# Modulation with the weights as stationary float32 blocks and two moving columns

## The chip, the core and the metric

The kernel runs on one core of a Trainium2 chip. A core has TensorE (matrix products, "PE" in the profile; its weight loads are listed apart as "PEld"), VectorE ("DVE"), ScalarE ("ACT"), GpSimd ("POOL") and SyncE ("SP"), which here only issues DMAs. The metric is the device time of one execution in microseconds (us), as a median of several runs.

## The reference, cut to what matters

One layer of a diffusion trunk is applied to 128 context tokens and 2048 grid tokens with the same weights. Each of the two token groups has its own condition vector of 1024 values. The part that the change touches is the modulation: `silu(cond) @ w_ada + b_ada`, with `w_ada` of 1024 x 6144, which gives six vectors of 1024 values for each group.

```python
mod = (jax.nn.silu(cond) @ w_ada + b_ada)[..., None, :]
shift1, scale1, gate1, shift2, scale2, gate2 = jnp.split(mod, 6, axis=-1)
h = rmsnorm(x, g_mix) * (1 + scale1) + shift1
p = h @ w_in
...                     # convolution, gated DeltaNet in two directions, Fourier mix
x = x + gate1 * (mix @ w_out)
h2 = rmsnorm(x, g_ffn) * (1 + scale2) + shift2
gt, up = jnp.split(h2 @ w_gu, 2, axis=-1)
x = x + gate2 * ((jax.nn.silu(gt) * up) @ w_down)
```

So shift1 and scale1 are needed before the first token can be normalised, and the other four only later: shift2, scale2 and gate1 at the end of the mixer, gate2 at the end of the SwiGLU part.

## The kernel before

All products are made to float32 accuracy. The large ones split each operand into a rounded part ("hi", float32r) and the rest ("lo"), and add three float32r products. The splitting is done by `split` (line 145): ScalarE rounds (line 150), and VectorE or, where the caller says so, GpSimd subtracts (line 151, through `tt`, line 130). A helper records each operation, so that nearly all matmuls have line 124, all transposes line 127, all ScalarE operations line 140.

The stages follow each other as functions:

- `setup` (line 188) loads constants and computes `silu(cond)`; it splits the two condition columns into four columns `cs4` (hi and lo of each) and two columns `cs2` padded to four.
- `phase_a` (line 353) is the pass over the tokens. It first runs `mod_columns(0, ...)` (line 367), which calls `mod_part` for shift1 and scale1. Between its steps it calls `load_halves` (line 343), which loads the key half of the input weights, and splits them. Then the 17 blocks of 128 tokens are normalised, transposed (`xn`), modulated to `h`, split to `hi` and `lo`, stored to HBM as `hT` and multiplied with the Fourier and gate columns of the input weights (`wfh`, `wfl`). From the fifth block on the loads and splits go on, one step a block.
- `gates` (line 406) computes the decay gates from all tokens with a few float32 products (`const_gates`).
- `qk_pass` (line 548) goes over 8 blocks of 256 tokens. For each it reloads `hT` (tiles `hb`) and makes 8 projections of 24 matmuls each, then a convolution (ScalarE makes `y` and `conv_in`, VectorE the two taps in `y`, line 137, ScalarE the silu to `kq`), and the products of keys and queries (`pair_products`, line 618, tiles `kq`, `sq`). Behind three of each four projections stands `next(self.mod, None)` (line 577): one step of the later modulation. `self.fill` (line 98) adds steps of the triangular inversion (tiles `inv_a`, `inv_b`, `inv_m`), which VectorE does alone.
- `v_pass` (line 767) does the same for the values and for `z`; there the modulation steps stand at line 782.
- `scan1` and `scan2` walk over the chunks of 64 tokens, and the Fourier part and the output product run beside them.
- `phase_d` (line 1303) is the SwiGLU part in three blocks of up to 768 tokens.

`mod_part` (line 231) handles one of the six vectors. It goes over two halves of 512 columns and, in each, over 8 blocks of 128 rows; one such block of 128 x 512 weights is called a step here, so a vector has 16 steps. A step loads the weights (one DMA for one or two steps, line 243), splits them (line 244), and makes two matmuls in which the condition columns are stationary (128 x 4) and the weights move (512 columns), lines 245 and 246. After 8 steps ScalarE copies the 4 x 512 result to `row`, four small transposes turn it to columns, and ScalarE copies them to `v` (lines 248 to 253). In the head the split weights lie in the tiles of the query half of the input weights (line 363), which is why that half is loaded only afterwards; later they have two tiles of their own, tagged `ada` (line 263), and GpSimd subtracts (line 375).

The order of the instructions on each engine is set by a scheduler that works from the program's order and from a timing model of its own (`schedule_with_timeline_sim=True`, line 1462). Each engine then runs its queue in that order, and a tile that is not free yet holds up the instruction that writes it. The pool `stage` (line 322) has 3 buffers of 4 KB a partition under the tag `st`, which all staged weight loads and `row` share. PSUM has three banks tagged `m` in these phases (line 313).

## Time and profile before

| | us |
|---|---|
| median of 3 runs | 2767.01 (2766.07 to 2773.3) |
| the profiled execution | 2767.64 |
| its span in the profile | 2765.8 |

The rows that the prediction uses stand in the section before it. In the windows, each engine has its busy time and, in brackets, the number of its instructions; PEclk is the granted clock of TensorE as a share of 2.4 GHz, so 0.50 is 1.2 GHz. A matmul is pipelined, so the duration of a single record is longer than its distance to the next, and the busy times of groups overlap. In a group of instructions the last columns are the busy time, the mean duration of one in ns, and the idle time of the engine ahead of them, with what ended it. Names like `acc<-hb,w_in` say what is written and what is read; `m<-w_ada,cs` are the later modulation's matmuls, `m<-w_in,cs` those of the head, whose split weights lie in tiles of `w_in`. A plain float32 matmul is listed as two records.

### The profile page before, as it was taken

Reading aid. Unit: us, or ns where it says so; the run is one execution under the profiler, and the core shown is the slowest. Engines: PE = TensorE matmul, PEld = TensorE weight load, DVE = VectorE, ACT = ScalarE, POOL = GpSimd, SP = SyncE. Lnnn points to the kernel's source line nnn. Section 1 sums busy time; section 2 is a strip of 40 time slices with the busy share of each in tenths; the row PEclk is TensorE's granted clock in tenths of the full one; section 3 lists DMA queues with packets and bytes.
Section 4 is the critical chain, followed back from the end, with each engine's and each line's share of the span. In section 5 each row is a group of like instructions: output and inputs, shape, how many; then the busy total and the mean of one; then the engine's idle time right before and its main releaser. Section 6 shows DMA issues by size and latency. Waiting matters only on the chain.

```text
span 2765.8 us, 44580 instructions
## 1 busy us (share of the span) xinstructions
PE 2610.3 (94%) x15769; PEld 2366.6 (86%) x15769; DVE 1971.7 (71%) x3860; ACT 1395.2 (50%) x3090; POOL 354.4 (13%) x486
## 2 busy tenths in 40 slices
PE   6999798899999899997999999999999999999998
PEld 3898687788888778876999998789999888999987
DVE  6335598998999677755877766577777556888744
ACT  7756454432277877765433344433434444444442
POOL 1214333431200012220000000020000002000001
PEclk8999898899999999998999999999999999999999
DMA  9946685555365666644322223532222253332342
GB/s 311 307 139 204 177 256 162 157 164 180 109 193 194 195 176 195 200 152 151 90 73 73 73 71 94 179 122 77 73 69 70 89 158 120 105 88 82 95 137 93
DMA packets 412283, 390.83 MB, mean 141 GB/s; under 512 B 99948, under 2 KB 335900, under 8 KB 411164
## 3 DMA queue, kind: packets, MB, share of 16 engines
q1 hardware_dynamic: 323996, 300.92, 36.1%
q10 hardware_dynamic: 74128, 40.13, 5.0%
q0 software_dynamic: 13936, 46.93, 4.9%
q8 instruction: 125, 2.05, 0.3%
q14 instruction: 98, 0.80, 0.1%
HBM read 293.55 MB, written 94.33 MB: 140 GB/s over the span
## 4 chain that ended last, share of the span: by engine, by line
issue 31%; PE 27%; DMA 2%; DVE 1%; ACT 1%; POOL 1%; ACTq 0%; POOLq 0%; SPq 0%; DVEq 0%
PE acc L124 9%; PE m L124 8%; PE acc L1273 5%; PE m L1273 5%; PE tr L127 1%; POOL rstd L130 1%; DMA z_s<-z_d 0%; DMA y_f<-half_d 0%; DMA half_d<-gy 0%; DVE x_f L137 0%; ACT h L140 0%; DVE x_f L130 0%; DMA bd1a<-a_d 0%; POOL y L1401 0%; DMA g<-gate_d 0%
## 5 line engine op out<-in xcount | busy, mean ns | idle before, releaser
L1273 PE MATMUL m<-h,wh 128*128 128x384 f32 (+1 forms) x1848 | 456.1, 329 | 14.5 <-ACT h L140 7.2
L1273 PE MATMUL acc<-h,wh 128*128 128x384 f32 (+1 forms) x1848 | 449.8, 327 | 0.0
L140 ACT ACTIVATE wh<-S 128x512 fp32r<-128x512 f32 x264 | 163.8, 630 | 376.5 <-DVE S L130 161.5
L124 PE MATMUL acc<-hb,w_in 128*128 128x258 f32 (+1 forms) x2304 | 333.6, 302 | 15.7 <-DMA hb<-hT 10.9
L1273 PEld LDWEIGHTS m<-h,wh 128*128 128x128 f32 x1848 | 328.4, 189 | 19.6 <-ACT h L140 8.9
L124 PEld LDWEIGHTS acc<-hb,w_in 128*128 128x128 f32 x2304 | 318.3, 199 | 26.8 <-issue 12.2
L1273 PEld LDWEIGHTS acc<-h,wh 128*128 128x128 f32 x1848 | 327.2, 189 | 1.0 <-ACT wh L140 0.4
L1273 PE MATMUL acc<-h,wl 128*128 128x384 f32 (+1 forms) x924 | 300.6, 327 | 6.0 <-DVE wl L130 6.0
L1273 PE MATMUL m<-h,wl 128*128 128x384 f32 (+1 forms) x924 | 302.3, 328 | 0.0
L140 ACT ACTIVATE wh<-w_gu 128x512 fp32r<-128x512 f32 x198 | 124.4, 630 | 118.8 <-issue 51.6
L130 DVE TENSOR_TENSOR wl<-S,wh 128x512 fp32r<-128x512 f32 x264 | 179.0, 686 | 5.3 <-ACT wh L140 3.1
L1273 PEld LDWEIGHTS acc<-h,wl 128*128 128x128 f32 x924 | 174.0, 189 | 6.9 <-DVE wl L130 6.9
L1273 PEld LDWEIGHTS m<-h,wl 128*128 128x128 f32 x924 | 174.9, 189 | 0.0
L140 ACT ACTIVATE awh<-a 128x384 fp32r<-128x384 f32 x176 | 90.7, 520 | 136.0 <-PE m L124 88.1
L130 DVE TENSOR_TENSOR awl<-a,awh 128x384 fp32r<-128x384 f32 x176 | 96.6, 555 | 87.1 <-ACT awh L140 87.0
L1387 POOL DMA_DIRECT2D half_d<-gy x17 | 9.3, 546 | 1160.9 <-DVE gy L130 1160.3
L130 DVE TENSOR_TENSOR wl<-w_gu,wh 128x512 fp32r<-128x512 f32 x198 | 135.4, 685 | 27.2 <-ACT wh L140 27.0
L130 DVE TENSOR_TENSOR S<-w_gu 128x512 f32<-128x512 f32 x132 | 91.1, 691 | 88.4 <-DMA w_gu<-w_gu 87.9
L137 DVE SCALAR_TENSOR_TENSOR y<-conv_in,wconv,y 128x256 f32<-128x256 f32 (+1 forms) x216 | 123.2, 584 | 39.7 <-ACT conv_in L140 39.1
L130 POOL TENSOR_TENSOR w_ada<-w_raw,w_ada 128x512 fp32r<-128x512 f32 x64 | 99.2, 1566 | 136.9 <-ACT w_ada L140 136.7
L124 PE MATMUL acc<-woh,mh 128*128 128x512 f32 x272 | 113.2, 419 | 3.0 <-DVE gx L130 2.9
L130 DVE TENSOR_TENSOR inv_b<-inv_b,inv_m 128x62 f32<-128x62 f32 (+30 forms) x124 | 114.1, 920 | 2.3
(281 smaller groups left out, 5927.9 us busy)
## 6 DMA issues: line engine op xcount, KB each, us to landing
w_gu<-w_gu SPq DMA_DIRECT2D x264, 256.0 KB
pk<-pk_d SPq DMA_DIRECT2D x68, 512.0 KB
w_dn<-w_down SPq DMA_DIRECT2D x132, 256.0 KB
hb<-hT SPq DMA_DIRECT2D x104, 258.0 KB
w_raw<-w_ada SPq DMA_DIRECT2D x32, 512.0 KB
x<-x SPq DMA_DIRECT2D x17, 512.0 KB
hT<-hi ACTq DMA_DIRECT2D x17, 512.0 KB
hT<-lo POOLq DMA_DIRECT2D x17, 512.0 KB, 6.1
```

The source lines that it names most:

```text
L124: self.nc.tensor.matmul(out, lhsT=lhsT, rhs=rhs, start=start, stop=stop)
L127: self.nc.tensor.transpose(out=out, in_=in_, identity=self.c("ident")[:in_.shape[0], :in_.shape[0]])
L130: (eng or self.nc.vector).tensor_tensor(out=out, in0=a, in1=b, op=op)
L137: self.nc.vector.scalar_tensor_tensor(out=out, in0=a, scalar=s, in1=b, op0=op0, op1=op1)
L140: self.nc.scalar.activation(out=out, in_=in_, func=f, **kw)
L1273: nc.tensor.matmul(o, lhsT=w_[:, ws], rhs=h_[:, k, :sub], start=start and k == i == 0, stop=k == 3 and i == 2, skip_group_check=not start)
L1387: nc.gpsimd.dma_start(self.half_d[n], tmp)
```

## The change

The weights are no longer split. Each 128 x 128 block of a step is loaded as it came, as float32, as the stationary operand, and the two condition columns move through it, so a step has four matmuls with two moving columns. The results are columns already: they add up in one PSUM bank for all 16 steps of a vector, which a product with a tile of zeros clears first (a step's matmuls only add). The copies to `row`, the small transposes and `v` fall away, and the columns are read from PSUM. The `ada` tiles are gone, and `stage` has 5 buffers in place of 3. In the head, the weights no longer use the tiles of the input weights, so the loads of both halves no longer stand between the steps or behind them: they are left to the token pass in the program.

```diff
--- before.py
+++ after.py
@@ -190,13 +190,10 @@
         self.cst = {}
         cond = const.tile([P, KT, 2], F32, name="cond")
         nc.sync.dma_start(cond, A["condT"])
-        cs = const.tile([P, KT, 2], F32, name="cs")
-        self.act(cs, cond, AF.Silu)
-        self.cs4 = const.tile([P, KT, 4], F32R, name="cs4")
-        self.cs2 = const.tile([P, KT, 4], F32R, name="cs2")
-        nc.vector.memset(self.cs2.bitcast(F32), 0.0)
-        self.split(self.cs4[:, :, 0:2], self.cs4[:, :, 2:4], cs)
-        nc.vector.tensor_copy(self.cs2[:, :, 0:2], cs)
+        self.cs = const.tile([P, KT, 2], F32, name="cs")
+        self.act(self.cs, cond, AF.Silu)
+        self.none = const.tile([P, 2 * KT], F32, name="none")
+        nc.vector.memset(self.none, 0.0)
         self.load_consts(const, "all")
         self.neg_half = self.small.tile([P, 1], F32, name="neg_half", bufs=1)
         nc.gpsimd.memset(self.neg_half, -0.5)
@@ -228,40 +225,33 @@
         self.h2_d = [d([P, KT, len(b) * P], F32, name=f"h2_d{i}") for i, b in enumerate(BLOCKS)]
         self.gate_d = d([2, 2, D], F32, name="gate_d")
 
-    def mod_part(self, part, tiles, bank, *engs):
+    def mod_part(self, part, raws, bank):
 
         nc, A = self.nc, self.A
-        v = self.small.tile([P, KT, 4], F32, tag="modv", name="modv", bufs=1)
+        ps = self.bank(bank)
+        self.mm(ps[:, :2 * KT], self.c("ident"), self.none)
         for a in range(0, D, 512):
-            ps = self.bank(bank)
             col = part * D + a
             for k in range(KT):
-                hi, lo, raw = next(tiles)
+                raw = next(raws)
                 w = raw.shape[1]
                 if k % w == 0:
                     src = A["w_ada"][k * P:(k + w) * P, col:col + 512]
                     nc.sync.dma_start(raw, src.rearrange("(k p) c -> p k c", p=P))
-                self.split(hi, lo, raw[:, k % w], *engs)
-                self.mm(ps[:4], self.cs4[:, k], hi, start=(k == 0), stop=False)
-                self.mm(ps[:4], self.cs2[:, k], lo, start=False, stop=(k == KT - 1))
+                for n in range(4):
+                    at = 2 * (a // P + n)
+                    nc.tensor.matmul(ps[:, at:at + 2], lhsT=raw[:, k % w, n * P:(n + 1) * P], rhs=self.cs[:, k],
+                                     start=False, stop=True, skip_group_check=True)
                 yield
-            row = self.stage.tile([4, 512], F32, tag="st", name="row")
-            self.act(row, ps[:4])
-            pt = self.bank("tr")
-            for n in range(4):
-                self.tr(pt[:, n * 4:n * 4 + 4], row[:, n * P:(n + 1) * P])
-            self.act(v[:, a // P:a // P + 4].rearrange("p k r -> p (k r)"), pt[:, :16])
         bias = self.b_ada[:, part * KT:(part + 1) * KT].unsqueeze(2).to_broadcast([P, KT, 2])
-        self.tt(v[:, :, 0:2], v[:, :, 0:2], v[:, :, 2:4], ALU.add)
-        return v[:, :, 0:2], bias
+        return ps[:, :2 * KT].rearrange("p (k r) -> p k r", r=2), bias
 
     def ada_tiles(self):
 
         while True:
             raw = self.stage.tile([P, 2, 512], F32, tag="st", name="w_raw")
             for _ in range(2):
-                w = self.stage.tile([P, 2, 512], F32R, tag="ada", name="w_ada", bufs=2)
-                yield w[:, 0], w[:, 1], raw
+                yield raw
 
     def mod_columns(self, which, *source):
 
@@ -319,7 +309,7 @@
     def phase_ab(self):
         nc, A = self.nc, self.A
         with ExitStack() as left:
-            self.stage = self.pool(left, "stage", 3, side="left")
+            self.stage = self.pool(left, "stage", 5, side="left")
             self.wp = self.pool(left, "w_in", side="left")
             wk = self.w_half(1)
             self.hb = self.pool(left, "hb", 16, side="left")
@@ -360,21 +350,17 @@
 
             def tiles():
                 while True:
-                    for hi, lo in zip(*self.w_half(0)):
-                        yield hi, lo, self.hb.tile([P, 1, 512], F32, tag="hb", name="w_raw")
-
-            qk = self.load_halves(wk, 512)
-            for i, _ in enumerate(self.mod_columns(0, tiles(), "m")):
-                if i % 8 == 4:
-                    next(qk)
+                    yield self.hb.tile([P, 1, 512], F32, tag="hb", name="w_raw")
+
+            self.run(self.mod_columns(0, tiles(), "m"))
             wq = self.w_half(0)
             wh = [wp.tile([P, FW], F32R, name=f"wfh{k}") for k in range(KT)]
             wl = [wp.tile([P, FW], F32R, name=f"wfl{k}") for k in range(KT)]
             for k in range(KT):
                 self.load_split(wh[k], wl[k], A["w_in"][k * P:(k + 1) * P, 2048:2048 + FW], FW, self.stage, "st")
-            rest = self.ada_tiles(), "m", nc.gpsimd
+            rest = self.ada_tiles(), "m"
             self.mod = chain(self.mod_columns(1, *rest), self.mod_gate(0, *rest), self.mod_gate(1, *rest))
-            qk = chain(qk, self.load_halves(wq, 0))
+            qk = chain(self.load_halves(wk, 512), self.load_halves(wq, 0))
             for n, t in enumerate([16] + list(range(16))):
                 rows = slice(t * P, (t + 1) * P)
                 x = work.tile([P, D], F32, tag="x", name="x")
```

The order on TensorE at the start. Before (`cs_67` is `cs4` and `cs_68` is `cs2`; the rows are those around the end of the first eight steps):

```order
L124 MATMUL m<-w_in,cs_67 4x512 x2
L124 MATMUL m<-w_in,cs_68 4x512 x2
L124 MATMUL m<-w_in,cs_67 4x512
L127 MATMUL tr<-const_all,row 128x4 x4
L124 MATMUL m<-w_in,cs_68 4x512
```

After, from the first matmul on:

```order
L124 MATMUL m<-none,const_all 128x16 x2
L243 MATMUL m<-cs,w_raw 128x2 x128
L127 MATMUL tr<-const_all,xn 128x128 x12
L124 MATMUL acc<-wfh_352,hi 128x264
L124 MATMUL acc<-wfl_360,hi 128x264
```

All 128 small matmuls of the 32 steps stand in one run ahead of the token pass's transposes.

The order of DMAs on SP in the head, from the first modulation weights on. Before (line 243 modulation weights, 348 halves of the input weights, 278 their Fourier and gate columns, 381 tokens):

```order
L243 DMA w_raw<-w_ada 128x512 x5
L348 DMA w_raw<-w_in 128x2x512
L243 DMA w_raw<-w_ada 128x512 x17
L348 DMA w_raw<-w_in 128x2x512
L243 DMA w_raw<-w_ada 128x512 x9
L381 DMA x<-x 128x1024
L243 DMA w_raw<-w_ada 128x512
L348 DMA w_raw<-w_in 128x2x512
```

After (240 modulation weights, 338 halves, 268 Fourier and gate columns, 367 tokens):

```order
L240 DMA w_raw<-w_ada 128x512 x20
L268 DMA w_raw<-w_in 128x528 x3
L240 DMA w_raw<-w_ada 128x512
L268 DMA w_raw<-w_in 128x528 x2
L240 DMA w_raw<-w_ada 128x512
L367 DMA x<-x 128x1024 x2
...
L338 DMA w_raw<-w_in 128x2x512
L240 DMA w_raw<-w_ada 128x512
L338 DMA w_raw<-w_in 128x2x512 x5
L240 DMA w_raw<-w_ada 128x2x512 x5
```

Twenty modulation loads stand in a row now; the Fourier and gate columns, four token blocks and all eight loads of the halves are mixed with the last twelve or follow them at once, ahead of the first `hT` reloads. On ScalarE and VectorE the 16 splits of the halves now stand ahead of the first modulated token block.

The order on TensorE in the middle of the query and key pass. Before:

```order
L124 MATMUL acc<-hb,w_in 128x258 x14
L124 MATMUL m<-w_ada,cs_67 4x512
L124 MATMUL m<-w_ada,cs_68 4x512
L124 MATMUL acc<-hb,w_in 128x258 x48
L124 MATMUL m<-w_ada,cs_67 4x512
L124 MATMUL m<-w_ada,cs_68 4x512
L124 MATMUL acc<-hb,w_in 128x258 x24
```

After:

```order
L124 MATMUL acc<-hb,w_in 128x258 x23
L243 MATMUL m<-cs,w_raw 128x2 x4
L124 MATMUL acc<-hb,w_in 128x258 x48
L243 MATMUL m<-cs,w_raw 128x2 x4
L124 MATMUL acc<-hb,w_in 128x258 x24
L243 MATMUL m<-cs,w_raw 128x2 x4
```

A step keeps its place behind three of four projections; its two matmuls become four, and they wait for the load alone.

## Rows read from the trace of the kernel before

**Rows 1.** The page's first part: busy time, share of the span, instructions.
```profile
PE 2610.3 (94%) x15769; PEld 2366.6 (86%) x15769; DVE 1971.7 (71%) x3860; ACT 1395.2 (50%) x3090; POOL 354.4 (13%) x486
```

**Rows 2.** Windows: stretch, its length, busy us per engine, PEclk, DMA share, GB/s.
```profile
0.00:46.00 46.00, 27.38 (x93) 8.08 (x94) 29.75 (x57) 34.24 (x67) 1.77 (x9) 0.85 0.87 304
46.00:180.00 134.00, 122.52 (x939) 118.55 (x940) 54.51 (x128) 96.09 (x207) 38.14 (x65) 0.95 0.89 279
180.00:300.00 120.00, 111.99 (x944) 101.75 (x942) 58.16 (x161) 68.39 (x145) 34.65 (x32) 0.99 0.51 152
300.00:880.00 580.00, 519.87 (x3794) 462.62 (x3795) 532.91 (x927) 273.58 (x644) 157.37 (x155) 0.94 0.60 177
1303.00:2750.00 1447.00, 1428.79 (x7763) 1334.21 (x7764) 1002.19 (x1729) 608.49 (x1136) 48.43 (x80) 0.99 0.32 97
```

**Rows 3.** Groups by line, operation and shape: count, busy us, mean ns, idle before.
```profile
L140 ACT ACTIVATE w_ada<-w_raw 128x512 fp32r<-128x512 f32 x64 | 39.0, 630 | 38.3 <-DMA w_raw<-w_ada 27.4 <-PE m L124 8.6 <-DVE r L662 2.0
L130 POOL TENSOR_TENSOR w_ada<-w_raw,w_ada 128x512 fp32r<-128x512 f32 x64 | 99.2, 1566 | 136.9 <-ACT w_ada L140 136.7
L124 PE MATMUL m<-w_ada,cs 128*4 128x512 f32 x128 | 45.5, 418 | 14.4 <-ACT w_ada L140 9.7 <-POOL w_ada L130 4.6
L124 PE MATMUL m<-const_all,sq 128*64 128x1 f32 x544 | 23.1, 206 | 3.0 <-DVE rows L676 2.1 <-ACT sq L140 0.9
L124 PE MATMUL m<-la,const_gates 128*128 128x68 f32 x8 | 1.1, 282 | 1.8 <-DVE la L130 1.8
```

**Rows 4.** The chain that ended last: start us, us, six 512-column matmuls.
```profile
1742.73 1.38 PE acc L124 x6
```

**Rows 5.** Timeline of TensorE: start us, us, operation, stationary rows x columns, moving.
```profile
23.35 0.41 PE L127 MATMUL tr<-const_all,row 4*128 4x4 f32 x4
...
38.03 0.59 PE L127 MATMUL tr<-const_all,row 4*128 4x4 f32 x4 [2.04 <-ACT row L140]
...
208.24 0.83 PE L124 MATMUL m<-la,const_gates 128*128 128x68 f32 x6
```

**Rows 6.** Timeline of three engines in the head.
```profile
6.68 0.63 ACT L140 ACTIVATE w_in<-w_raw 128x512 fp32r<-128x512 f32 x1 [3.75 <-DMA w_raw<-w_ada]
...
41.40 0.17 DVE L130 TENSOR_TENSOR mod_cols<-mod_cols,gains 128x16 f32<-128x16 f32 x1
...
45.74 0.59 PE L124 MATMUL acc<-wfh,hi 128*128 128x264 f32 x1 [0.59 <-ACT hi L140]
```

**Rows 7.** Windows around changes of the granted clock.
```profile
18.55:35.62 17.07, 13.97 (x54) 3.17 (x53) 14.83 (x26) 14.96 (x31) 0.74 (x2) 1.00 1.04 390
35.62:49.27 13.65, 7.76 (x33) 6.17 (x33) 9.88 (x23) 11.92 (x25) 1.77 (x3) 0.50 0.70 219
25.38:28.79 3.41, 2.28 (x8) 0.43 (x7) 3.41 (x7) 3.41 (x8) 0.00 (x0) 1.00 1.05 395
489.58:493.00 3.42, 2.52 (x55) 2.36 (x56) 3.35 (x9) 3.35 (x9) 1.52 (x2) 1.00 0.89 281
493.00:496.41 3.41, 3.41 (x18) 3.41 (x17) 3.41 (x5) 1.45 (x3) 2.92 (x2) 0.50 0.36 109
```

**Rows 8.** Groups by line: 209 to 640, 680 to 755, and 300 to 640 us.
```profile
L137 DVE SCALAR_TENSOR_TENSOR y<-conv_in,wconv,y 128x256 f32<-128x256 f32 x128 | 81.1, 637 | 31.3 <-ACT conv_in L140 31.0
...
L137 DVE SCALAR_TENSOR_TENSOR y<-conv_in,wconv,y 128x256 f32<-128x256 f32 x24 | 11.4, 478 | 0.0
...
L130 POOL TENSOR_TENSOR w_ada<-w_raw,w_ada 128x512 fp32r<-128x512 f32 x48 | 77.3, 1627 | 117.9 <-ACT w_ada L140 117.7
```

**Rows 9.** Timeline of GpSimd and VectorE around 588 us.
```profile
586.99 3.47 POOL L130 TENSOR_TENSOR w_ada<-w_raw,w_ada 128x512 fp32r<-128x512 f32 x2 [17.48 <-ACT w_ada L140]
587.92 2.82 DVE L137 SCALAR_TENSOR_TENSOR y<-conv_in,wconv,y 128x127 f32<-128x127 f32 x2
```

**Rows 10.** Waits, 209 to 680 us: us in total, times, longest.
```profile
ACT kq L140 <- DVE y L137: 58.1, 31, 6.9
...
ACT w_ada L140 <- DMA w_raw<-w_ada: 27.4, 3, 19.9
```

## The prediction

> **What bounds the kernel now.** I read the page's shares first: TensorE is busy 94% of the span [rows 1]. Such a share is a mean over stages, so the second view is the busy time by stretches [rows 2], in which the reader should compare TensorE with VectorE. In 1303 to 2750 us (the SwiGLU part) TensorE is busy 1428.79 of 1447 us and nothing of the change lies there. In 300 to 880 us, VectorE is busy 532.91 of 580 us and TensorE 519.87: two engines share that stretch, and it is where most of the modulation's second share runs. In 0 to 46 us neither is full (27.38 and 29.75 us): that is the head, which waits for the first 32 steps of the modulation. So there are three places to price: the head, the token pass behind it (46 to 180 us), and 180 to 880 us.
>
> **The change part by part.** A step is one 128x512 block of the modulation weights; there are 96, of which 32 in the head and 64 later. *Removed* for each step: one ScalarE rounding copy (0.63 us), one subtraction (VectorE in the head, GpSimd later, 1.57 us there) and two matmuls with 512 moving columns [rows 3]. Such matmuls follow each other every 0.23 us at the full clock (1.38 us for six, [rows 4]), so two cost 0.46 us. Per 8 steps a row copy, four small transposes (0.41 us, [rows 5]) and a copy back go too, and in their place stands one matmul that clears the bank per 16 steps. *Added* for each step: four float32 matmuls with a 128x128 stationary block and 2 moving columns.
>
> No row shows that form. What a float32 matmul is in the trace: line 650 issues 34 x 2 x 4 = 272 of them and the trace has 544 records [rows 3], so each is two load-and-multiply pairs. The nearest row with a full float32 stationary block and few columns is the gates' sums with 68 columns: six records take 0.83 us, the last of them its own 0.28 us, so one starts every 0.11 us [rows 3, 5]. From below: the 64-column blocks with one column take 23.1 us for 544 records, 0.04 us each [rows 3], but they fill half of the array's columns. From above: 0.83/6 = 0.14 us. I take 0.11 us, since that row has the same stationary block and a block with 2 columns must still be loaded. A step then costs 4 x 2 x 0.11 = 0.90 us of TensorE at the full clock against 0.46 us before: +0.44 us (bounds -0.1 and +0.66).
>
> *Head.* The first weights have landed at 6.68 us, when ScalarE begins to split them; the modulation columns are ready at 41.57 us and the first matmul of the token pass starts at 45.74 us [rows 6]. Afterwards the order puts all 128 blocks in one run on TensorE, ahead of everything else. What counts is the clock. Two short stretches of equal length tell: from 25.38 us TensorE was busy 2.28 us with 512-column matmuls and the clock stayed at 2.4 GHz (1.00) until 35.62 us; from 489.58 us it was busy 2.52 us, mostly with kq and sq products of one to 128 columns on half-width blocks, and from 493.00 us it was granted 0.50, which is 1.2 GHz [rows 7]. Being busy with loads did not hold the clock there. A run of 2-column blocks that begins from an idle engine therefore, I take it, stays at the lower level. The four small transposes, nearly all weight load, took 0.59 us at 38.03 us, at that level, and 0.41 us at 23.35 us, at the higher [rows 5, 7], so the load slows with the clock, and I double 0.11 to 0.215 us: 256 records x 0.215 = 55 us, from 6.7 to about 62 us. Transposes, h and its split then take about 3 us (4.2 us before, [rows 6]): the first matmul of the pass at about 65 us, **+19 us**. At the full clock the run would be 28 us and end at 35 us; then the DMAs set the end. What the SP order puts ahead of the pass, about 17 MB (8.4 modulation weights, 2.2 and 4.2 input weights, 2.1 tokens), takes 43 us at the 395 GB/s of a full stretch [rows 7]; with the 6.68 us in which the first of it came, the first matmul would stand at about 50 us: +4 us.
>
> The Trainium skill, page "TensorE: Matmul & The Clock Gate", section "LDWEIGHTS (loading the stationary operand)", gives a load as columns / 1.2, 107 ns for 128, with no word of the clock. By that alone the head's run would be about 27 us. The 0.41 and 0.59 us of the small transposes say that the load does depend on the level, so I don't use it. The same page, Part 1, "What's actually happening", says that the clock follows how busy the engine was; by it a run without gaps should come up to 2.4 GHz, which is the second rival below. The stretch from 489.58 us, busier than the one that kept its clock, speaks against it.
>
> *Token pass, 46 to 180 us.* TensorE is idle 11.5 of 134 us, and a mean clock of 0.95 means some 13 us at half speed, another 6.7 us lost [rows 2]. All eight input-weight loads with their 16 splits, the eight Fourier and gate loads and the first two normalised token blocks are now done while TensorE runs the head, which takes work from ScalarE and VectorE here. I count **-10 us** (0 to -18).
>
> *180 to 300 us.* 16 steps x 0.44 = 7 us; TensorE is idle 8 us here [rows 2] and the first 20 blocks stand in the wait for the gates: **+4 us** (0 to +8).
>
> *300 to 880 us.* 48 steps. TensorE gets 48 x 0.44 = 21 us less 2 us for the transposes: 519.87 + 19 = 539 us. VectorE does none of these steps, yet gains: while GpSimd subtracts, VectorE's two-input operations stand still. The convolution's 128x256 operation takes 637 ns on average between 209 and 640 us, where the subtractions lie (48 of them behind 300 us), and 478 ns behind 680 us, where there is none [rows 8]; over 128 operations that is 20 us in one group alone. One place shows it whole: two subtractions, 3.47 us, and beside them two 128x127 operations that take 2.82 us [rows 9]; a 256-wide one takes 0.48, so at least 1.86 us went, 0.9 us a subtraction. Between 20 us over 64 subtractions, 0.3, and 0.9 us I take 0.8, near the direct row: 48 x 0.8 = 38 us less, 495 us. If TensorE sets the stretch at the 97% that it reaches elsewhere (98.7% in the last row of [rows 2]), it is 539/0.97 = 556 us, -24 us; if VectorE does at its present 92%, 538 us, -42 us. ScalarE, which waited 58.1 us for VectorE's convolutions before its kq copies and 27.4 us for modulation weights [rows 10], loses 30 us of copies too. I take **-30 us**. A new wait comes with it: TensorE now waits for the weight DMA itself, and the projections stand queued behind the block; before, ScalarE's copies took that wait. Five stage buffers in place of three hide it; uncovered it would be up to those 27.4 us.
>
> Sum: +19 - 10 + 4 - 30 = -17 us on the profiled execution's 2767.64 us (2765.8 us span), which lies 0.02% above the median 2767.01: **2750 us**.
>
> **The rivals.** *TensorE is the bound of 180 to 880 us (slower).* The mechanism: VectorE's freed time only becomes waiting for projections, because each in the queue stands behind a block. For it: TensorE's 519.87 us are nearly VectorE's. Against it: the waits of ScalarE for VectorE. Price: +19 - 5 + 8 + 19 = +41 us at the full price, 2808; with a third of the gain on VectorE left, 2795. It decides if TensorE's busy share in the 300-us stretch stays at 0.90 or below while VectorE's falls under 0.85. *The clock comes up in the head.* Pass starts at 50 us, +4, with 5 recovered instead of 10: -1 + 4 - 30 = -27 us, 2741. *VectorE was the whole bound.* -42 in place of -30: 2738; with the clock up as well 2729. *They cancel.* With 0.3 us a subtraction in place of 0.8 VectorE gives 14 us, and with -10 in place of -30 the sum is +3: 2770.
>
> **How the numbers follow.** Forecast (2740 to 2760) 0.38; clock up 0.15; VectorE the whole bound 0.13; cancel 0.13; TensorE bound 0.21. About 0.3%, 8 us, can be told from no change. Faster: 0.34 of the first and the next two, 0.62. Same: the rest of the first and most of the cancelling case, 0.16. Slower: 0.22. The range goes down to 2716, below both gains together, and up to 2790, which leaves out half of the slow rival.
>
> **What would show it.** Records of 2-column matmuls 0.21 us apart at a granted 0.50 in the head, and the first matmul with the token weights near 65 us; 0.11 us apart and near 50 would be the second rival. The convolution's 128x256 operation near 480 ns between 209 and 640 us. A stretch that ended at 880 us before now ends near 863 us; if it ends behind 890, the slow rival is right. The SwiGLU part should be as long as before; if it changes by more than some us, something else moved. The prediction is wrong as a whole if the float32 pair takes much over 0.14 us at the full clock, or if VectorE's operations stay slow with GpSimd idle.

## The result: slower by 0.8%, and the profile after

The changed kernel takes 2791.38 us (median of 4 runs, 2785.6 to 2796.37), the kernel before 2767.26 us beside it; ratio 1.0082, 95% interval 1.0057 to 1.0107. In a second set it took 2791.2 us (5 runs, 1.0071, 1.0057 to 1.0084). The forecast of 2750 us had the wrong sign, and the time lies outside the range by a little. The profiled execution is the longest of its four, 2796.37 us with a span of 2794.6, so the trace shows some 5 us more than the median.

The page's first part of after, columns as in [rows 1]:

```profile
PE 2665.9 (95%) x16309; PEld 2465.7 (88%) x16309; DVE 1900.2 (68%) x3820; ACT 1340.6 (48%) x2969; POOL 257.9 (9%) x422
```

TensorE has 55.6 us more work, VectorE 71.5 us less, GpSimd 96.5 us less. Windows of after, cut where TensorE has the same matmuls behind it as in [rows 2], apart from the modulation's own (300 us before and 339 us after lie in a pause of TensorE behind the 576th matmul `acc<-hb,w_in`; only four kq products have changed sides):

```profile
0.00:65.00 65.00, 58.38 (x272) 57.82 (x272) 17.88 (x33) 22.06 (x38) 1.76 (x9) 1.00 0.85 304
65.00:198.00 133.00, 123.01 (x961) 119.56 (x960) 46.69 (x115) 88.78 (x193) 35.54 (x63) 0.99 0.79 242
198.00:339.00 141.00, 126.27 (x1036) 121.91 (x1034) 59.33 (x168) 60.94 (x123) 14.77 (x17) 0.89 0.54 149
339.00:898.00 559.00, 526.68 (x4036) 491.90 (x4036) 485.71 (x921) 249.96 (x591) 83.26 (x108) 0.94 0.62 184
1333.00:2780.00 1447.00, 1429.26 (x7769) 1333.45 (x7770) 1003.50 (x1731) 609.02 (x1138) 48.48 (x80) 0.99 0.32 97
```

The head is 19 us longer, the token pass as long as before (133 against 134 us), the stretch of 120 us takes 141, the long one of 580 takes 559, and the SwiGLU part is unchanged. What is missing from these rows, 898 to 1333 us, is the scan's second part: 435 us in place of 423.

The blocks themselves. Groups by line of after (count, busy us, mean ns, idle before), in place of the w_ada rows of [rows 3]:

```profile
L243 PEld LDWEIGHTS m<-cs,w_raw 128*128 128x128 f32 x768 | 128.0, 259 | 2.2 <-issue 2.1
L243 PE MATMUL m<-cs,w_raw 128*128 128x2 f32 x768 | 126.3, 294 | 2.0 <-DMA w_raw<-w_ada 2.0
```

96 steps x 4 blocks x 2 records = 768, as counted; TensorE waited 2.0 us for these weights in all, so the wait that the prediction feared (27.4 us) didn't come. The timeline of TensorE in after (start us, us, operation, stationary, moving), which answers to [rows 5, 6]:

```profile
6.72 54.74 PE L243 MATMUL m<-cs,w_raw 128*128 128x2 f32 x256 [1.98 <-DMA w_raw<-w_ada]
...
65.17 0.59 PE L124 MATMUL acc<-wfh,hi 128*128 128x264 f32 x1
...
235.15 4.27 PE L243 MATMUL m<-cs,w_raw 128*128 128x2 f32 x20
...
333.44 0.95 PE L243 MATMUL m<-cs,w_raw 128*128 128x2 f32 x8
...
551.87 11.72 PE L243 MATMUL m<-cs,w_raw 128*128 128x2 f32 x60
```

In the head 256 records take 54.74 us, 0.214 each. At 235.15 us 20 records take 4.27 us, 0.214 each as well, and there the trace shows a granted 0.50 (first window below); at 333 us, at a granted 1.00, eight take 0.95 us, 0.119 each. So the head ran at TensorE's lower level, 1.2 GHz. (The windows show 1.00 for the head only because the trace's first record of the clock comes at 68.53 us; for the stretch ahead of it the durations speak.) The 60 records at 551.87 us belong to a run of 35 blocks; the second window, around it, has a mean granted clock of 0.56 with TensorE busy throughout, and answers to the last row of [rows 7]:

```profile
228.90:239.20 10.30, 10.30 (x51) 10.27 (x50) 3.00 (x10) 8.14 (x13) 0.00 (x0) 0.50 0.29 79
551.70:565.40 13.70, 13.70 (x72) 13.70 (x72) 12.85 (x26) 2.87 (x8) 2.50 (x1) 0.56 0.82 235
```

VectorE's convolution in after, from 209 to 660 us (group, count, busy us, mean ns, idle before), where [rows 8] has a mean of 637 ns:

```profile
L137 DVE SCALAR_TENSOR_TENSOR y<-conv_in,wconv,y 128x256 f32<-128x256 f32 x134 | 67.7, 510 | 50.2 <-ACT conv_in L140 49.7
```

So the mean falls to 510 ns, most of the way to the 478 ns that it had before only where GpSimd made no subtractions. Yet the wait of ScalarE for it is no shorter than the 58.1 us of [rows 10]. Waits of after, 209 to 704 us:

```profile
ACT kq L140 <- DVE y L137: 72.2, 35, 14.0
```

### The profile page after: what moved, and what is told of

It is laid out like the page before. It is cut to its first block, busy times and chain, and to the rows that moved or that the text cites. A ratio compares the mean times of both kernels' runs of the same rounds, so it can differ in the third digit from the quotient of the medians.

```text
span 2794.6 us, 45389 instructions
## 1 busy us (share of the span) xinstructions
PE 2665.9 (95%) x16309; PEld 2465.7 (88%) x16309; DVE 1900.2 (68%) x3820; ACT 1340.6 (48%) x2969; POOL 257.9 (9%) x422
## 4 chain that ended last, share of the span: by engine, by line
PE 54%; DVE 3%; DMA 3%; ACT 3%; issue 1%; POOL 1%; ACTq 0%; SPq 0%; DVEq 0%; POOLq 0%
PE acc L1259 16%; PE m L1259 15%; PE acc L124 11%; PE m L124 11%; DMA z_s<-z_d 1%; DMA y_f<-half_d 1%; ACT bd1r L140 0%; ACT h L140 0%; DVE x_f L137 0%; PE tr L127 0%; DVE S L130 0%; ACT o_part L140 0%; POOL rstd L130 0%; DVE h L130 0%; ACT u L140 0%
## 5 line engine op out<-in xcount | busy, mean ns | idle before, releaser
L124 PE MATMUL acc<-hb,w_in 128*128 128x258 f32 (+1 forms) x2304 | 328.0, 301 | 7.9 <-ACT conv_in L140 7.9
L124 PEld LDWEIGHTS acc<-hb,w_in 128*128 128x128 f32 x2304 | 312.2, 198 | 10.2 <-ACT conv_in L140 8.7
L130 DVE TENSOR_TENSOR awl<-a,awh 128x384 fp32r<-128x384 f32 x176 | 96.5, 556 | 91.4 <-ACT awh L140 91.3
L137 DVE SCALAR_TENSOR_TENSOR y<-conv_in,wconv,y 128x256 f32<-128x256 f32 (+1 forms) x216 | 101.4, 484 | 70.1 <-ACT conv_in L140 64.2
L243 PEld LDWEIGHTS m<-cs,w_raw 128*128 128x128 f32 x768 | 128.0, 259 | 2.2 <-issue 2.1
L243 PE MATMUL m<-cs,w_raw 128*128 128x2 f32 x768 | 126.3, 294 | 2.0 <-DMA w_raw<-w_ada 2.0
```

The lines of the kernel that those rows point to most:

```text
L124: self.nc.tensor.matmul(out, lhsT=lhsT, rhs=rhs, start=start, stop=stop)
L130: (eng or self.nc.vector).tensor_tensor(out=out, in0=a, in1=b, op=op)
L137: self.nc.vector.scalar_tensor_tensor(out=out, in0=a, scalar=s, in1=b, op0=op0, op1=op1)
L243: nc.tensor.matmul(ps[:, at:at + 2], lhsT=raw[:, k % w, n * P:(n + 1) * P], rhs=self.cs[:, k], start=False, stop=True, skip_group_check=True)
```

## The experiments

Every run but the first of after was timed in five rounds beside the kernel before (2768.9 to 2772.3 us there). The table is read from each trace's timeline of TensorE: the first matmul with the token weights, the last one (end of the pass), the first S matmul (start of the scan), the last output matmul (its end). "Late" is from the end of the pass to the start of the scan and holds all 64 later steps. Each kernel has one trace; after and after_again are the same kernel, and their traces differ by 3.4 us in the pass and 9.8 us in late, so a difference of that size between two single traces shows nothing by itself. The diffs below are cut to the lines that matter.

```
kernel          time     ratio, interval          first   pass end  scan from  late    scan
before          2767.3   1                         45.7    180.3     756.7     576.4   536.4
after           2791.4   1.0082 (1.0057, 1.0107)   65.2    197.9     773.3     575.4   547.5
after_again     2791.2   1.0071 (1.0057, 1.0084)   65.2    201.3     766.9     565.6   549.7
old_head        2773.7   1.0018 (1.0007, 1.0029)   45.9    184.7     754.3     569.6   547.2
old_late        2786.6   1.0061 (1.0048, 1.0075)   65.0    201.6     777.9     576.3   536.1
moving_head     2763.2   0.9975 (0.9965, 0.9986)   43.7    186.7     757.1     570.4   530.1
no_sub          2746.1   0.9919 (0.9907, 0.9930)   46.2    177.9     721.0     543.2   553.2
half_late       2764.7   0.9975 (0.9964, 0.9985)   65.2    200.3     751.6     551.3   537.9
scan_order      2774.9   1.0015 (1.0006, 1.0024)   65.0    200.1     772.8     572.7   525.3
scan_before     2774.1   1.0019 (1.0010, 1.0027)   65.4    199.2     769.0     569.8   529.9
moving_all      2754.2   0.9942 (0.9927, 0.9956)   43.7    183.4     743.7     560.3   531.1
moving_old      2787.6   1.0062 (1.0047, 1.0076)   44.1    196.3     771.8     575.5   535.1
wf_early        2754.9   0.9945 (0.9929, 0.9961)   43.5    178.8     749.7     570.9   527.4
old_head_order  2759.2   0.9975 (0.9963, 0.9988)   46.3    181.3     755.1     573.8   527.4
```

**The two halves of the change, each alone.** old_head:

```diff
-            self.run(self.mod_columns(0, tiles(), "m"))
+            qk = self.load_halves(wk, 512)
+            for i, _ in enumerate(self.mod_columns_split(0, tiles(), "m")):   # mod_part of before
+                if i % 8 == 4:
+                    next(qk)
```

> The kernel after, but the first 32 steps of the modulation by the scheme of before (rounded weights as 512 moving columns, two matmuls a step); the 64 later steps stay with stationary float32 blocks. Theory A (the head's TensorE run at 1.2 GHz costs 19 us and nothing behind it gives that back): first token matmul near 46 us, time 2791 - 19 = 2772 us, so 5 us above before. Theory B (the prediction's terms behind the head hold, -36 us, and something else was lost): near 2731 us. Theory C (what ScalarE and VectorE did during the longer head is now late): 2780 us or more.

2773.7 us, and the first token matmul at 45.9: theory A. By the medians the new head costs 18 us. In the traces the first token matmul of after stands 19 us later than here, and only the pass behind it gives a little of that back (132.7 and 136.1 us in the two traces of after, 138.8 here); late and scan are the same within their scatter.

old_late:

```diff
-            rest = self.ada_tiles(), "m"
+            rest = self.ada_tiles(), "m", nc.gpsimd      # ada tiles and mod_part of before, stage of 3
```

> The kernel after, but the 64 later steps by the scheme of before (GpSimd subtracts, two 512-column matmuls); the head stays with stationary float32 blocks. Theory A (TensorE sets 180 to 770 us, so the new late steps win and lose about the same): before plus the head, 2767 + 19 = 2786 us. Theory of the prediction (the late steps won 30 us): 2791 + 26 = about 2815 us. If the late steps were the loss and the head were not: 2770 us.

2786.6 us, theory A's 2786. The prediction's 30 us for the late steps would have shown here as 2815; the late half of the change, with all that hangs on it in the program, gains nothing and costs some 5 us by the medians, though the intervals of the two ratios overlap. That the sum comes out so is in part chance: old_late's late is 1 to 11 us longer than in the two traces of after, and its scan 11 to 14 us shorter, for a reason that comes further down.

**Why the head is slow.** moving_head turns the operands round: the weights move as they are, float32, and the condition is stationary (in a copy of `mod_part` that only the head calls; here against `mod_part`).

```diff
-                for n in range(4):
-                    at = 2 * (a // P + n)
-                    nc.tensor.matmul(ps[:, at:at + 2], lhsT=raw[:, k % w, n * P:(n + 1) * P], rhs=self.cs[:, k],
-                                     start=False, stop=True, skip_group_check=True)
+                self.mm(ps[:2], self.cs[:, k], raw[:, k % w], start=(k == 0), stop=(k == KT - 1))
                 yield
+            row = self.stage.tile([2, 512], F32, tag="st", name="row")      # then turned, as before
```

> The kernel after, but in the head the weights move: 32 plain float32 matmuls with the two condition columns stationary and 512 moving columns, rows copied and turned as before. Both forms take nearly the same TensorE work at 2.4 GHz (0.85 against 0.90 us a step by four passes a column). Theory A (it is the lack of streamed columns that keeps the clock at 1.2 GHz in the head): a granted 1.00 after the first records, steps 0.85 us apart or as the weights arrive, first token matmul near 50 us, time about 2791 - 15 = 2776 us. Theory B (the clock stays low there whatever runs): steps 1.7 us apart, 55 us for the 32, first token matmul near 65 us, 2791 us.

2763.2 us, 28 below after and 0.25% below before. The head's timeline of TensorE in moving_head (two records a matmul):

```profile
7.38 14.77 PE L124 MATMUL m<-w_raw,cs 128*2 128x512 f32 x30 [7.38 <-DMA w_raw<-w_ada]
...
22.42 6.17 PE L124 MATMUL m<-w_raw,cs 128*2 128x512 f32 x14
```

14 records are 7 steps in 6.17 us, 0.88 us a step; the first 15 come as their weights arrive, 0.98 us apart, with the DMAs full in the window:

```profile
7.00:22.00 15.00, 14.62 (x30) 2.66 (x30) 0.00 (x0) 0.59 (x1) 0.00 (x0) 1.00 1.04 381
```

Here the trace has records of the clock from 10.91 us on, at 1.00 until 41.63. The two forms have nearly the same TensorE work at 2.4 GHz (0.88 us a step against 8 x 0.119 = 0.95), both keep TensorE busy from the first weight on, and one stands at the lower level, the other at the higher. What TensorE did differs: here each load of two columns is followed by 512 moving columns, in after each load of 128 columns by two. Of the two theories the clock and the step bear out A. The pass starts at 43.7, not 50; I take it that not all the input weights need be there for its start. That the time is 13 us below theory A's is luck: between the two traces the head gives 21.5 us, of which the pass takes 10.3 back (143.0 us in place of 132.7); late gives 5, within its scatter, and the scan 17.4, by an order that the scheduler wrote, of which more below.

**VectorE's relief and TensorE's price, one at a time.** no_sub, from the kernel before:

```diff
-                self.split(hi, lo, raw[:, k % w], *engs)
+                if engs:                       # the 64 later steps
+                    self.act(hi, raw[:, k % w])
+                    lo = hi
+                else:
+                    self.split(hi, lo, raw[:, k % w])
```

> The kernel before, without GpSimd's 64 late subtractions: the second matmul of a late step takes the rounded weights instead of what the rounding left, so the low part of the late modulation is not computed. TensorE, ScalarE and the DMAs do what they did; only the sharing of GpSimd and VectorE goes. Theory A (VectorE's relief is worth only the TensorE idle time that it removes, about 50 - 28 = 22 us between the first kq and the last projection): -15 to -22 us, 2745 to 2752 us. Theory of the prediction (0.8 us a subtraction on the path): 64 x 0.8 = 51 us at most, 38 at least: 2716 to 2729 us. Rival (the sharing lies beside other work): 2767 us.

By the time, 2746.1 us, theory A; by the trace, neither. The scan starts at 721.0, 36 us earlier than before, and late takes 543.2 in place of 576.4 us: the relief is 33 us, close to the prediction's 38. By the medians the time fell by only 23, in this trace by 15, since the scan is 17 us longer. Not all of the 33 need be the sharing: TensorE also waited 4.6 us for GpSimd's results themselves [rows 3], and that wait is gone too. Three parts of the stretch 300 to 880, windows of before:

```profile
300.00:534.00 234.00, 199.09 (x1805) 179.68 (x1806) 203.92 (x392) 116.83 (x231) 88.60 (x67) 0.88 0.71 195
534.00:757.00 223.00, 209.34 (x1247) 183.47 (x1245) 211.52 (x262) 66.24 (x161) 63.93 (x76) 0.98 0.47 150
757.00:880.00 123.00, 111.45 (x750) 99.47 (x749) 117.46 (x275) 90.52 (x252) 4.84 (x13) 0.97 0.64 190
```

the same work in no_sub, with the stretch ahead of it (180 to 300 us before) in the first line:

```profile
178.00:299.00 121.00, 111.34 (x940) 100.74 (x938) 50.00 (x162) 66.71 (x142) 15.44 (x18) 0.99 0.52 152
299.00:509.00 210.00, 186.80 (x1809) 170.12 (x1809) 175.61 (x392) 117.41 (x234) 38.48 (x35) 0.93 0.78 219
509.00:721.00 212.00, 203.95 (x1243) 179.29 (x1239) 192.78 (x260) 66.59 (x161) 37.14 (x60) 0.99 0.49 155
721.00:845.00 124.00, 114.19 (x756) 102.44 (x756) 118.73 (x277) 90.13 (x254) 6.54 (x13) 0.94 0.63 191
```

and in after, where the stretch ahead is the 141 us from 198 to 339 shown above:

```profile
339.00:551.00 212.00, 196.36 (x1973) 191.97 (x1973) 184.96 (x401) 98.91 (x196) 40.90 (x36) 0.92 0.72 208
551.00:773.00 222.00, 216.94 (x1326) 197.86 (x1323) 195.66 (x260) 56.65 (x140) 37.07 (x60) 0.95 0.45 142
773.00:898.00 125.00, 113.38 (x744) 102.08 (x744) 105.08 (x262) 94.40 (x255) 5.29 (x15) 0.93 0.73 217
```

Ahead of 300 us the relief is worth nothing (120 and 121 us), and with the blocks the stretch takes 141. Of the three parts, the first comes down from 234 to 210 without the subtractions and stays at 212 with the blocks: there TensorE had room for them. The second comes down from 223 to 212 and goes back up to 222, with TensorE busy 216.94 us, 97.7%. The third has no step and no subtraction, and hardly moves. (In after_again the stretch ahead takes 138 us, the first two parts 210 and 218.)

half_late takes TensorE's side, from after:

```diff
-                for n in range(4):
+                for n in range(4 if w == 1 else 2):      # w is 1 in the head
```

> The kernel after with two of the four float32 matmuls of each of the 64 later steps left out (half of the later modulation is not computed); weights still arrive whole. TensorE gives up 64 x 0.45 = 29 us. The scan's order falls as in before. Theory A (TensorE sets 180 to 770 us): the scan starts 25 to 35 us earlier, at 738 to 748 us in place of 773, and the time is 2791 - 29 - 15 (the scan's order) = 2747 us. Theory of the prediction carried over (VectorE sets half of it): the scan starts 10 us earlier at most, time 2766 us.

The scan starts at 751.6, 22 us earlier than in after; late takes 551.3 us where the seven kernels with all blocks have 565.6 to 575.4 (mean 571). So 20 of the 29 us given up were on the path, against the mean. By late that is between the theories, nearer to A (25 to 35) than to the other (10); the time, 2764.7, is 18 above A's and 1 below the other's, mostly since late gave 9 us less than A said and the scan 10 in place of 15. Neither theory is borne out whole. The stretch ahead, where after has 141 us, still takes 137 with half the blocks.

Together: late is 576 us in the three kernels with GpSimd's subtraction, 543 in one trace without it, and 571 in the mean of the seven traces with the blocks. So the gain is 33 us, the price 571 - 543 = 28, and 5 us remain. By the count the steps add the same 64 x 0.44 = 28 us on TensorE, but that the two agree is partly chance: half_late, with TensorE's late steps back at before's work, keeps 8 us of the price, and by place 17 to 20 us of it lie ahead of 300 us, for 18 steps that count for 8, and only 6 to 12 behind, for the other 46.

**The scan that was not touched.** In the table the scan takes 535 to 538 us in four kernels, 547 to 553 in four, 525 to 531 in six. On TensorE the scan's instructions stand in the same order within each of the first two groups from its second half on, and five of the last group share another (scan_before is the sixth); the change has moved none of them in the program. The scheduler writes the outputs' matmuls between the steps of the state by its own reckoning of when each is ready, and that reckoning starts from what came ahead. scan_order tests it:

```diff
         self.bd = {}
+        pad = oacc.tile([P, 512], F32, name="pad")
+        for _ in range(2):
+            nc.gpsimd.memset(pad, 0.0)
```

> The kernel after, with two GpSimd memsets of an unused 128x512 tile at the scan's start. Up to the scan no instruction of TensorE moves; in the scan the scheduler then writes the outputs' matmuls between the state's steps in the order of moving_head instead of that of after (the last 1281 of the scan's TensorE instructions stand as there). Theory D (the scan of after is longer because of the order in which it was written: 547 us in the trace of after, 530 in that of moving_head): -15 to -17 us, 2774 to 2776 us, scan starting at 773 us as before. Theory E (the scan's length differs from one execution to the next by chance of the clock, whatever its order): 2791 us, within its 5 us.

2774.9 us: theory D. Two memsets that compute nothing take 16 us off. scan_before, one memset of 128x1:

> The kernel after with one GpSimd memset of an unused 128x1 tile at the scan's start. Up to the scan no instruction of TensorE moves; the end of the scan then stands in the order of before (its last 243 TensorE instructions; in after only the last 11 agree). Theory D (the written order sets the scan's length; the traces so far have 535 to 538 us in the order of before, 547 to 553 in that of after, 525 to 531 in that of moving_head): scan 536 us, time 2791 - 11 = 2780 us, and what is left above before, 11 us, is the change itself. Theory E (only the order of moving_head is special): 2791 us.

2774.1 us. That the order sets the length is borne out; the size is not, 17 us and not 11. Only its last 243 instructions are those of before, and what is ahead of them took 482 us where before has 486 and after 493. after_again is after unchanged:

> The kernel after, unchanged, a second time: its first profiled execution was the longest of its four (2796 us, median 2791), so the 547 us of its scan may be chance. Theory D (the written order sets the scan's length): the scan takes 540 us or more again, the median is 2788 to 2793 us, and scan_order and scan_before stay some 15 us below it. Theory E (chance): the scan takes about 530 us in this trace, and the median comes down to 2780 us or less.

549.7 us and 2791.2: theory D. Windows over the scan: after,

```profile
773.00:1321.00 548.00, 509.05 (x2956) 437.98 (x2956) 374.85 (x1089) 393.43 (x1121) 72.61 (x146) 0.97 0.59 179
```

and scan_order:

```profile
773.00:1298.00 525.00, 498.41 (x2950) 434.49 (x2949) 368.76 (x1084) 392.81 (x1120) 70.25 (x136) 0.99 0.61 184
```

The same work takes 10.6 us more of TensorE's time at a clock of 0.97 in place of 0.99, and 12 us more are idle. Part of the idle is one wait. TensorE's waits in that stretch (total us, times, longest), after:

```profile
PE m L124 <- ACT u L140: 12.6, 13, 4.2
```

and scan_order:

```profile
PE m L124 <- ACT u L140: 6.3, 14, 0.7
```

A step of the state whose input ScalarE hands over late stands for up to 4.2 us in one order and 0.7 in the other; in after_again it is 11.5 us in all and 3.8 at most. That the falls of the clock follow from such gaps is argued, not shown.

**Towards a faster kernel.** moving_all has the later steps in the moving form too (`mod_part` of moving_head everywhere):

> moving_head, with the 64 later steps in the same form too: one plain float32 matmul of 512 moving columns a step (0.88 us in the head of moving_head against 0.90 for four stationary blocks), rows copied by ScalarE and turned. If the block runs at 1.2 GHz are a loss of their own (35 blocks behind 536 us take 0.21 us a record there): the scan starts 5 to 10 us earlier than in moving_head (757 us), time 2754 to 2758 us. If the late steps cost only their TensorE time: as moving_head, 2763 us. If the row copies and turns stand in the way: 2768 us.

2754.2 us, 0.58% below before, in the range of the first theory. In its trace late is 10 us shorter than in moving_head, and no long run of blocks at the lower level stands there: the mean granted clock from pass to scan is 0.98 in place of 0.94. But wf_early, with the same later steps, has 0.96 and yet 570.9 us of late, and two traces of one kernel differ by as much, so that the 10 us come from the clock isn't settled. wf_early:

```diff
+            wf = (self.load_split(wh[k], wl[k], A["w_in"][k * P:(k + 1) * P, 2048:2048 + FW], FW, self.stage, "st")
+                  for k in range(KT))
+            for i, _ in enumerate(self.mod_columns(0, tiles(), "m")):
+                if i % 4 == 2:
+                    next(wf, None)
```

> moving_all with the eight loads and splits of the Fourier and gate columns of the input weights put between the head's steps, one each fourth step, in place of behind them; a 128x1 memset keeps the scan's order that of moving_head. In moving_all TensorE waits 17.4 us in the token pass (10.0 in after), and the DMA queue is at 90 to 170 GB/s for some 8 us around 35 to 42 us and full behind 55 us. Theory F (the input weights come late behind a shorter head): the pass starts within 2 us of 43.7 and is 5 to 7 us shorter, 2747 to 2750 us. Theory G (the queue is full in the whole, so the loads only push the modulation's weights back): the pass starts 3 to 5 us later and ends as before, 2754 us.

The pass does start at 43.5 and is 4.3 us shorter (135.4 against 139.7), nearly as theory F has it, but the time is that of G, 2754.9: late is 10.6 us longer, within what two traces differ by, and that gives the gain back.

moving_old is the head of moving_head with the later steps and the three stage buffers of before:

> The head of moving_head with the later steps of before (GpSimd subtracts, two 512-column matmuls). The scan's order is that of before. The late terms of before and after nearly cancel (old_head is 5 us above before, of which some 11 are the scan's order), so by theory A this kernel starts its scan within 5 us of before's 757 and takes 2763 to 2769 us. If the late steps with stationary blocks were the gain in moving_head: 2772 us or more.

2787.6 us, far outside. Late is 575.5 us as in the other kernels with subtractions; the miss is all in the token pass, which takes 152.2 us from 44.1 on (143.0 in moving_head, 134.6 in before). With a short head the loads and splits of all input weights fall into the pass, here through three buffers in place of five. Whether it is the buffers wasn't tried.

old_head_order joins the head of before, the late blocks and a better scan, by one memset of 128x1024 at the place of scan_order's:

> old_head with one GpSimd memset of an unused 128x1024 tile at the scan's start; the last 1900 TensorE instructions of the scan then stand as in scan_order. If the parts add up (head +18 us, the scan's order of after against that of scan_order +16 us, late steps -5 us against before), the head of before with the late steps of after and the scan order of scan_order takes 2791 - 18 - 16 = 2757 us, about 12 us less than before. If the late steps gain nothing: 2762 us or more. If the scan order was worth its 16 us only behind the longer head: 2774 us.

2759.2 us, 2 us from the sum and 0.25% below before: head and scan order add up. The late steps' 5 us can't be told from nothing, since 2759.2 lies 2 us from the one figure and 3 from the other.

## Why the prediction was wrong

- **Head, +19: right**, in number and in mechanism. First token matmul at 65.17 in place of 45.74, +19.4; 0.214 us a record against 0.215, at the lower level. The Trainium skill, page "TensorE: Matmul & The Clock Gate", section "LDWEIGHTS (loading the stationary operand)", gives columns / 1.2, by which 128 columns take an estimated 107 ns; the 0.119 us at the higher level come near it, the 0.214 of the head do not.
- **Token pass, -10: failed.** It took 132.7 and 136.1 us in the two traces of after, 134.6 before. I added TensorE's 11.5 us idle and 6.7 us for a low clock as if the input weights' splits were behind both. With the splits gone from the pass, TensorE still works 123.01 us where it worked 122.52, at 0.99 in place of 0.95, and is idle 10. Why its busy time didn't fall with the low clock gone, no run shows. Of the idle time the waits tell; TensorE's in the pass (total us, times, longest), before:

```profile
PE tr L127 <- ACT h L140: 3.8, 3, 1.4
...
PE acc L124 <- ACT wfh L140: 0.7, 1, 0.7
```

and after:

```profile
PE tr L127 <- ACT h L140: 6.2, 4, 2.3
```

Only 0.7 us of the idle time was for an input weight, and the wait for the modulated tokens grew by 2.4. The view of waits by what ended them, over the pass alone, would have told that part beforehand.

- **180 to 300, +4 (0 to +8): failed.** The same work takes 141 and 138 us in the two traces of after where it took 120: +21 and +18. I counted 16 steps at the higher level, 7 us, less some of TensorE's idle time, and let the first 20 blocks hide in the wait for the gates. They ran from 230.5 to 239.4 us at a granted 0.50, at the 0.214 us that I had used for the head and not here, and outlasted the wait: the first kq product starts 41.4 us behind the pass in place of 34.9 (239.3 - 197.9 against 215.2 - 180.3). The rest stays open: over the whole stretch the granted clock is 0.89 in place of 0.99, but leaving out half of the blocks saves only 1 to 4 us (half_late, 137 us, also at 0.89), and no run parts the clock from the rest.
- **300 to 880, -30: nearly right**, -21 and -26 (559 and 554 us). TensorE has 526.68 us (predicted 539), VectorE 485.71 (495); the relief by no_sub, 33 us in all, lies in this stretch, against the 38 counted. The result is near the -24 of "If TensorE sets the stretch at the 97%", but not by one limit for the whole: in the first part the relief stays nearly whole beside the blocks, in the second the blocks take it back, and in the third, which I had divided by 0.97 as well, there was nothing to win, with TensorE at 91% before and after. For 180 to 880 as a whole the prediction has -26, the traces 0 and -8.
- **The scan: not in the sum.** I looked only for work that moved. +11 and +13 us in the two traces of after came from an order that the scheduler rewrote behind the change.
- **The slow rival** (2795 to 2808) had the right sign, not by its cause. Its condition, TensorE at 0.90 or below and VectorE below 0.85, was not met (0.94 and 0.87), and of its +41 the +19 for the long stretch didn't come. The point that was 880 us does lie near 898, past its 890 (the Fourier matmuls of the scan start at 796.4 in place of 778.5 and end at 952.3 in place of 933.4), but by the head and the stretch to 300.

So the steps that failed are the pass's -10 (0 measured), the +4 ahead of 300 us (+18 to +21), and the scan, held at 0 (+12); the -30 was some 4 to 9 us too good. By the two traces of after the sum is +19.5 for the head, 0 for the pass, -5 for late (mean of the seven traces with blocks), +12 for the scan and +2 behind it, 28; these two executions are 2 to 5 us above their medians, which are 22 to 24 us above before.

## What to carry to other kernels

Where two engines share a stretch, don't price it by their two new totals: split it, and ask in each part what each edit gains or costs there. Here the relief of VectorE was worth nothing ahead of 300 us, was kept in the part behind it and was taken back in the next. Cut the traces of two kernels where the same instructions are done, and not at round times, before two stretches are compared. A block of weights that is used for two columns pays for its load, and here a run of such blocks stood at the lower clock and paid nearly twice (0.214 us a record against 0.119); with the larger operand moving, the head ended 21.5 us earlier. And where a scheduler writes the order, time a variant that differs only in that order before a per cent is put down to the change.

## What was not expected of the hardware

A plain float32 matmul with 512 moving columns takes 0.88 us at the higher level (7 in 6.17 us), nearly four times the 0.23 us of one with rounded operands [rows 4], and saves both the rounding copy and the subtraction. In the head of after TensorE was busy for 54.74 us without a gap, and by the distance of its records it stood at its lower level all the time. One GpSimd subtraction of 128x512 cost the kernel 33/64 = 0.5 us on the path (one trace of no_sub, with TensorE's own wait for it in the number), though its own 1.57 us [rows 3] lay beside other work.
